# A seven-product FFN: when the operand sums of its second half are split, and how long split weights are held

## The chip, the cores and the metric

The kernel runs on one NeuronCore of a Trainium2 chip. The metric is the device time of one execution in microseconds. One execution was also recorded by the profiler; its "span" is the time from its first to its last instruction on the core.

## The reference

One layer of a hybrid decoder is computed for 2048 prompt tokens and 64 sample tokens, in float32: RMSNorm, a joint input projection, sliding-window attention beside an RWKV-7 recurrence, a gated merge with a residual add, and then the causal ConvFFN with another residual add and a last RMSNorm. The change lies in the FFN alone:

```python
def conv_ffn(h, conv_prev, w_in, cw, cb, w_out):
    T = h.shape[1]
    u = h @ w_in
    gp, vp = u[..., :D_FF], u[..., D_FF:]
    buf = jnp.concatenate([conv_prev.astype(gp.dtype), gp], axis=1)
    c = cb + sum(cw[j] * buf[:, j:j + T] for j in range(CONV_W))
    return (jax.nn.gelu(c, approximate=True) * vp) @ w_out, buf[:, -(CONV_W - 1):]
# x = x + merged @ w_out
# f, conv_new = conv_ffn(rmsnorm(x, norm_ffn), conv_prev, w_ffn_in, ffn_conv_w, ffn_conv_b, w_ffn_out)
# D_MODEL = 1024, D_FF = 2816 (22 tiles of 128), CONV_W = 3
```

## The kernel before, in words

The 2112 tokens are worked in three blocks of 704. Features lie on the 128 partitions and tokens along the free dimension. Each block passes through input projections, attention and recurrence, a merge, and the FFN. Blocks 0 and 2 take the path of `stage_s`, which calls `merge_s` (L1231) and then `ffn_s` (L1307); block 1 takes the plain path `merge` and `ffn`, which the change doesn't touch.

**Precision by splitting.** Every matmul operand is stored as two parts, `hi`, a rounded copy, and `lo`, the value less that copy. `split` (L248) makes them: ScalarE (ACT) casts the value to `hi` (L249), then VectorE (DVE) or GpSimd (POOL) subtracts (L250). `unit` (L234) does the same for a 128 x 1024 weight: a load on SyncE's queue into the pool `wr` (two buffers), the cast by ACT at L241 into the pool `wp` (two buffers), the subtraction by DVE or POOL at L245. `mm3` (L252) multiplies hi by hi, hi by lo and lo by hi: three matmuls for each of the k-tiles, all at L260. A product of four k-tiles is 12 matmuls.

**Background work.** `push` hands a generator to a named stream. `mm3` calls `tick` ahead of the k-tiles whose number is 0, 3 or 6, and a tick advances each stream by one step; a value that the generator yields is a number of ticks to leave out. A product of four k-tiles ticks twice. `drain` runs what is left of a stream.

**Seven products.** In `ffn_s` the normalized input is cut in four: the two halves of its features by the two halves of the tokens (352 each, `FH`). The first token half gives t11 and t12, split into `sa` (a11, a12); the second gives t21 and t22. For each of the 22 feature tiles f, gate and value weights, also cut by halves of the features, are combined so that seven products of four k-tiles do instead of eight: a11 and a12 with the gate weight as it is (`wa`, or in the early loop `unit`), and five others with sums of weights, "quarters" (`quarter`, L1345, tile `wq`, three buffers; the sums, L1327, in tiles `tq` and `rw`), against the operand sums s2, s3, s1, a22 and s4. These five live in the tile `sb`, as parts 0 to 4: t11 (after it has been overwritten), t21, s1, t22 and t12. `p1`, `u2`, `u3` are partial results that DVE adds up out of PSUM.

**Order in a stage.** `merge_s` ends with the out-projection of both token halves, during which `first` makes `sa`. It then pushes `second` (L1281), which takes the norm of the second half and, for each k-tile, forms the operand sums on DVE and POOL, splits part 0, and at last splits parts 1 to 4: 20 splits of 128 x 352 in all, 10 with POOL. `second` is advanced by the ticks of the early loop (L1354): for f = 0 to 5 (`PRE` = 6) the products with a11 and a12, kept in `keep`. `t11` lies in `wq` buffers, `t21` in the tiles `gb` and `cc`, `t22` in `xv`, `s1` in `up` and one of the two buffers of `rw`, `t12` in `early`.

Then the main loop runs over groups of f (`GRP`: one of 2, five of 4). For each f it issues, in this order: for f of 6 and over the a11 product into the bank `bx` (L1382), with a copy `p1` of it by ACT (L1384); the product with s2 (`bw`); if a group has just ended, `behind()` (L1394), which is `ffn_out` (L1204) of that group; the products with s3 (`bz`) and s1 (`by`); for f of 6 and over the a12 product, added into `bx` (L1407); the copy of `c11` to `gb` and the first convolution tap (L1408, L1409); the products with a22 and s4, the convolution (L1194), the gelu (L1425), the product of gate and value (L1430) and the split into `ff`. `ffn_out` of a group of 4 takes four `unit` weights, each for 48 matmuls. `whole` (L1338) makes `wa[f + 1]` near the end of f, in a `wp` buffer.

**What sets the order on the engines.** The program is written with tiles; a planner takes the instructions in the order of the program as their rank, lets one go ahead where by its own estimates of cost the earlier ones aren't ready and a buffer is free, and writes one fixed queue for each engine. On the chip each engine works its queue in order and waits where the data or a buffer isn't there.

Of the kernel before, what the change touches and what calls it, by code (L numbers as in the profile page):

```python
# [26 lines left out]
FH = ((0, 352), (352, 352))  # L27
PRE = 6
# [76 lines left out]
class Kernel:  # L105
# [1125 lines left out]
    def merge_s(self, b, xp, msp, after):  # L1231

        nc = self.nc
        with self.pool("br") as brp:
            x, ms = self.branches(b, xp, brp, msp, brp)
        fp, sap, sbp = after()
# [42 lines left out]
        sb = sbp().tile([P, 5, 4, 2, n], F32R, name="sb")  # L1279

        def second():  # L1281

            part = lambda u, k, t, eng: self.split(sb[:, u, k, 0], sb[:, u, k, 1], t, eng)
            yield from rms(1)
            yield
            for k in range(4):
                normed(t21[k], k, 1)
                normed(t22[k], k + 4, 1)
                nc.vector.tensor_tensor(s1[k], t21[k], t22[k], op=ALU.add)
                nc.gpsimd.tensor_tensor(t21[k], t11[k], t21[k], op=ALU.subtract)  # L1290
                nc.vector.tensor_tensor(t11[k], s1[k], t11[k], op=ALU.subtract)
                part(0, k, t11[k], nc.gpsimd)
                nc.gpsimd.tensor_tensor(t12[k], t12[k], t11[k], op=ALU.subtract)
                yield
            for k in range(4):
                part(1, k, t21[k], nc.vector)
                if k % 2:
                    yield
            for u, t in ((2, s1), (3, t22), (4, t12)):
                for k in range(4):  # L1300
                    part(u, k, t[k], nc.gpsimd if k % 2 else nc.vector)
                yield

        self.push("m", second())
        return x, sa, sb, early

    def ffn_s(self, b, x, sa, sb, early, fp, between, done):  # L1307
        nc = self.nc
# [36 lines left out]
        def quarter(f, u):  # L1345
            if f < FF:
                t = raw[f][u]
                w = q[f, u] = fp.tile([P, 2, 512], F32R, tag="wq", name="wq", bufs=3)
                nc.scalar.copy(w[:, 0], t)  # L1349
                sub(nc.gpsimd, w[:, 1], t, w[:, 0].bitcast(F32))  # L1350
# [3 lines left out]
        for f in range(PRE):  # L1354
# [8 lines left out]
            nc.vector.tensor_tensor(c11, p1, pss[1][:, :n], op=ALU.add)  # L1363
        self.drain("m")
        quarter(0, 1)
        behind = None
        for f0, nf in GRP:
            ff = []
            for u in range(nf):
# [21 lines left out]
                u2 = self.tmp("u2")[:, :n]  # L1391
                nc.vector.tensor_tensor(u2, p1, bw[:, :n], op=ALU.add)
                if behind:
                    behind()  # L1394
                    behind = None
# [9 lines left out]
                nc.vector.tensor_tensor(up[:, n:], u3, by[:, :n], op=ALU.add)  # L1405
                if f >= PRE:
                    self.mm3(bx, wa.pop(f), a12, 0, n, nk=4, wk0=4, start=False)  # L1407
                nc.scalar.copy(gb[:, 2:2 + n], c11)  # L1408
                tap(c[:, :n], c11)  # L1409
                sums(f + 1)  # L1410
# [4 lines left out]
                if last:  # L1415
                    v8 = lambda t: t.rearrange("p (b i) -> p b i", i=8)
                    nc.vector.tensor_tensor(sv[:, :, 2:], v8(u2[:, np_:]), v8(bz[:, np_:n]), op=ALU.add)
                    tap(v8(c[:, npr:]), sv[:, :, 2:])
                whole(f + 1)
                quarter(f + 1, 0)  # L1420
# [173 lines left out]
    def stage_s(self, b, held, ahead=None):  # L1594
# [3 lines left out]
        with ExitStack() as es, ExitStack() as right:  # L1598
# [11 lines left out]

            x, sa, sb, early = self.merge_s(b, xp, msp, after)
            fp = pools[0]
# [29 lines left out]

            self.ffn_s(b, x, sa, sb, early, fp, between, self.final_last(b, x, fp) if last else self.final(b, x, FH))
            if last:
# [111 lines left out]
```

## Time and profile before

| what | value |
|---|---|
| three timed runs | 3622.6, 3636.28, 3649.86 us (median 3636.28) |
| the profiled execution | 3638.56 us |
| its span | 3636.8 us |
| TensorE (PE) matmul, busy | 3285.3 us, 90% of the span, 23544 matmuls |
| weight loads (PEld), busy | 3117.5 us, 86% |
| DVE, ACT, POOL, busy | 2276.3 (63%), 1290.5 (35%), 1398.3 us (38%) |
| mean granted TensorE clock | 0.956 of full |

A row of the timeline gives start in us, length, engine, line, operation, tile written and tiles read, shape and count; in brackets stands the idle time of the engine before it and what ended that. PEld are weight loads, SPq is SyncE's queue, where the loads are issued. In a row of a group of lines the numbers behind the first bar are busy us and mean ns of one, behind the second the idle time before them, by what ended it. A row on a tile gives minimum, median and maximum ns, and first and last start. Matmul records overlap, so their mean length is longer than the step from one to the next. Products into the banks `psd` and `psr` are told apart by what they read: `sa` (a11, a12), `sb` (the five others), `ff` (output products).

### The profile page before, as it was taken

What the parts mean: (1) busy time and instruction counts of PE and PEld (TensorE: products, weight loads), DVE (VectorE), ACT (ScalarE), POOL (GpSimd) and SP (SyncE); (2) the same over time, 40 slices, a digit from 0 to 9 for tenths busy, and PEclk for the clock granted to TensorE, in tenths of its full rate; (3) what the DMA queues carried; (4) which work ended last, traced back from release to release, by engine and by line L of the source; (5) the groups of instructions that cost most, each with busy time, mean ns of one, the idle gap of its engine ahead of it and who ended that gap; (6) DMA issues with size and microseconds to landing.
All of it is one profiled execution on the core that took longest, in us unless ns stands there. A gap on an engine that the chain in (4) does not pass through costs nothing. (4 is left out here: it accounts for less than half of the span.)

```text
span 3636.8 us, 61117 instructions
## 1 busy us (share of the span) xinstructions
PE 3285.3 (90%) x23544; PEld 3117.5 (86%) x23544; DVE 2276.3 (63%) x4739; ACT 1290.5 (35%) x2486; POOL 1398.3 (38%) x1224
## 2 busy tenths in 40 slices
PE   8888899988997899899899899999999997898987
PEld 7887788887896888898888689999999997798887
DVE  6668856579557755555665955564644656855555
ACT  4323533235333433333333432331222323433334
POOL 3443224342256444554344213122212345644445
PEclk9999899999998999999999899999999998999998
DMA  3444465544532312127545434433222463212122
GB/s 129 120 121 132 120 202 151 158 133 118 195 127 87 96 62 67 64 71 224 178 141 164 117 125 166 157 102 103 72 70 70 147 223 105 76 59 69 59 65 80
DMA packets 318708, 429.60 MB, mean 118 GB/s; under 512 B 83664, under 2 KB 242256, under 8 KB 318160
## 3 DMA queue, kind: packets, MB, share of 16 engines
q1 hardware_dynamic: 314256, 419.92, 37.1%
q10 hardware_dynamic: 4160, 5.77, 0.5%
q8 instruction: 186, 3.05, 0.4%
q14 instruction: 106, 0.87, 0.1%
HBM read 328.16 MB, written 98.41 MB: 117 GB/s over the span
## 5 line engine op out<-in xcount | busy, mean ns | idle before, releaser
L260 PE MATMUL psd<-h,wp 128*128 128x384 f32 (+2 forms) x6336 | 1168.8, 338 | 20.1 <-ACT wp L241 7.9
L260 PEld LDWEIGHTS psd<-h,wp 128*128 128x128 f32 x6336 | 1057.0, 196 | 41.3 <-ACT wp L241 8.2
L245 POOL TENSOR_TENSOR wp<-wr,wp 128x1024 fp32r<-128x1024 f32 x182 | 444.3, 2441 | 980.7 <-ACT wp L241 936.4
L260 PE MATMUL psd<-ff,wp 128*128 128x352 f32 (+2 forms) x3168 | 552.5, 331 | 48.9 <-POOL wp L245 23.8
L260 PEld LDWEIGHTS psd<-ff,wp 128*128 128x128 f32 x3168 | 517.3, 192 | 70.0 <-POOL wp L245 29.3
L260 PE MATMUL psd<-o,wp 128*128 128x384 f32 (+1 forms) x3264 | 544.4, 326 | 8.7 <-ACT wp L241 2.5
L260 PEld LDWEIGHTS psd<-o,wp 128*128 128x128 f32 x3264 | 529.6, 190 | 13.2 <-ACT wp L241 2.6
L241 ACT CAST wp<-wr 128x1024 fp32r<-128x1024 f32 x298 | 312.0, 1047 | 553.6 <-PE psd L260 434.0
L1220 DVE TENSOR_TENSOR x<-x,psd 128x352 f32<-128x352 f32 (+2 forms) x288 | 148.4, 518 | 273.5 <-PE psd L260 273.3
L260 PE MATMUL psd<-sb,wq 128*128 128x352 f32 x1584 | 283.5, 328 | 20.4 <-POOL wq L1314 17.5
L260 PEld LDWEIGHTS psd<-sb,wq 128*128 128x128 f32 x1584 | 263.2, 191 | 25.3 <-POOL wq L1314 21.6
L1314 POOL TENSOR_TENSOR wq<-tq,wq 128x512 fp32r<-128x512 f32 x132 | 191.5, 1453 | 205.2 <-ACT wq L1349 205.1
L260 PE MATMUL psr<-sb,wq 128*128 128x352 f32 x1056 | 205.5, 341 | 47.0 <-DVE u L1401 29.9
L260 PEld LDWEIGHTS psr<-sb,wq 128*128 128x128 f32 x1056 | 182.7, 199 | 55.6 <-ACT ff L249 19.1
L1194 DVE SCALAR_TENSOR_TENSOR cc<-gb,pt,cc 128x704 f32<-128x704 f32 (+1 forms) x132 | 182.4, 1382 | 22.0 <-ACT cc L1181 11.7
L245 DVE TENSOR_TENSOR wp<-wr,wp 128x1024 fp32r<-128x1024 f32 x116 | 153.0, 1319 | 52.5 <-ACT wp L241 51.5
L1314 POOL TENSOR_TENSOR wq<-rw,wq 128x512 fp32r<-128x512 f32 x88 | 132.7, 1508 | 67.4 <-ACT wq L1349 67.4
L1314 DVE TENSOR_TENSOR tq<-rw 128x512 f32<-128x512 f32 x88 | 86.8, 990 | 98.9 <-DMA rw<-in_w_fi 85.1
L260 PE MATMUL psr<-sa,wp 128*128 128x352 f32 x768 | 136.1, 324 | 0.7 <-ACT p L1384 0.7
L260 PEld LDWEIGHTS psr<-sa,wp 128*128 128x128 f32 x768 | 125.5, 188 | 1.9 <-ACT p L1384 1.9
L250 DVE TENSOR_TENSOR ff<-cc,ff 128x352 fp32r<-128x352 f32 (+2 forms) x132 | 111.4, 853 | 21.1 <-ACT ff L249 18.9
L844 DVE TENSOR_TENSOR m<-psr,ct 128x512 f32<-128x512 f32 (+2 forms) x88 | 46.0, 542 | 111.4 <-DMA kbd<-kt 55.6
(318 smaller groups left out, 4654.6 us busy)
## 6 DMA issues: line engine op xcount, KB each, us to landing
wr<-in_w_in SPq DMA_DIRECT2D x108, 512.0 KB, 3.8
wr<-in_w_fi SPq DMA_DIRECT2D x100, 512.0 KB, 3.5
wr<-in_w_fo SPq DMA_DIRECT2D x70, 512.0 KB, 3.5
rw<-in_w_fi SPq DMA_DIRECT2D x44, 512.0 KB, 3.5
wr<-in_w_out SPq DMA_DIRECT2D x40, 512.0 KB, 3.5
cm<-md SPq DMA_DIRECT2D x33, 512.0 KB, 4.7
gt<-gd SPq DMA_DIRECT2D x48, 352.0 KB, 4.3
md<-m SPq DMA_DIRECT2D x48, 256.0 KB, 3.2
```

Of the source, the lines that this page charges most:

```text
L241: nc.scalar.copy(w[:, 0], raw)
L245: eng.tensor_tensor(w[:, 1], raw, w[:, 0].bitcast(F32), op=ALU.subtract)
L250: (eng or self.nc.vector).tensor_tensor(lo, src, hi.bitcast(F32), op=ALU.subtract)
L260: nc.tensor.matmul(ps[:, :n], w[:, a, wk * 128:(wk + 1) * 128], x, skip_group_check=not start, start=(start and k == 0 and j == 0), stop=( ...
L844: nc.vector.tensor_tensor(m[:, :kpr], ps[:, :kpr * 128].rearrange("p (c j) -> p c j", j=128), self.cst("maskp").unsqueeze(1).to_broadcast( ...
L1194: nc.vector.scalar_tensor_tensor(c[:, :npr], gb[:, u:u + npr], cw[u], c[:, :npr], op0=ALU.mult, op1=ALU.add)
L1220: nc.vector.tensor_tensor(xv, xv, ps[:, :n], op=ALU.add)
L1314: sub = lambda eng, o, p, q: eng.tensor_tensor(o, p, q, op=ALU.subtract)
```

## The change

Two things change in the two seven-product stages. First, `second` splits only part 0, with DVE instead of POOL, and each k-tile takes two steps with a tick left out after each. The splits of the other four parts become four callables, which `ffn_s` calls around f = 0: part 1 (t21) right behind the early loop, part 2 (s1) behind the s2 product, part 3 (t22) behind the s1 product and part 4 (t12) behind the a22 product; in each, DVE and POOL take turns (t21 was split by DVE alone). Second, where a group has just ended and f is 6 or over, the a12 product, the copy to `gb` and the first tap go ahead of `behind()`, so that `wa[f]` is given up before the group's output products instead of after them.

```diff
@@ merge_s
         sb = sbp().tile([P, 5, 4, 2, n], F32R, name="sb")
+        part = lambda u, k, t, eng: self.split(sb[:, u, k, 0], sb[:, u, k, 1], t, eng)
+
         def second():
-            part = lambda u, k, t, eng: self.split(sb[:, u, k, 0], sb[:, u, k, 1], t, eng)
             yield from rms(1)
             yield
             for k in range(4):
@@
                 nc.gpsimd.tensor_tensor(t21[k], t11[k], t21[k], op=ALU.subtract)
+                yield 1
                 nc.vector.tensor_tensor(t11[k], s1[k], t11[k], op=ALU.subtract)
-                part(0, k, t11[k], nc.gpsimd)
+                part(0, k, t11[k], nc.vector)
                 nc.gpsimd.tensor_tensor(t12[k], t12[k], t11[k], op=ALU.subtract)
-                yield
+                yield 1
+
+        def rest(u, t):
             for k in range(4):
-                part(1, k, t21[k], nc.vector)
-                if k % 2:
-                    yield
-            for u, t in ((2, s1), (3, t22), (4, t12)):
-                for k in range(4):
-                    part(u, k, t[k], nc.gpsimd if k % 2 else nc.vector)
-                yield
+                part(u, k, t[k], nc.gpsimd if k % 2 else nc.vector)
 
         self.push("m", second())
-        return x, sa, sb, early
+        return x, sa, sb, early, [lambda u=u, t=t: rest(u + 1, t) for u, t in enumerate((t21, s1, t22, t12))]
@@ ffn_s
         self.drain("m")
+        parts[0]()
         quarter(0, 1)
@@
                 nc.vector.tensor_tensor(u2, p1, bw[:, :n], op=ALU.add)
+                if f == 0:
+                    parts[1]()
                 if behind:
+                    if f >= PRE:
+                        self.mm3(bx, wa.pop(f), a12, 0, n, nk=4, wk0=4, start=False)
+                        nc.scalar.copy(gb[:, 2:2 + n], c11)
+                        tap(c[:, :n], c11)
                     behind()
                     behind = None
@@
                 nc.vector.tensor_tensor(up[:, n:], u3, by[:, :n], op=ALU.add)
-                if f >= PRE:
+                if f == 0:
+                    parts[2]()
+                if f in wa:
                     self.mm3(bx, wa.pop(f), a12, 0, n, nk=4, wk0=4, start=False)
-                nc.scalar.copy(gb[:, 2:2 + n], c11)
-                tap(c[:, :n], c11)
+                if f < PRE or u:
+                    nc.scalar.copy(gb[:, 2:2 + n], c11)
+                    tap(c[:, :n], c11)
                 sums(f + 1)
@@
+                if f == 0:
+                    parts[3]()
                 whole(f + 1)
```

`stage_s` passes the four callables from `merge_s` on to `ffn_s`.

More of the change, by code (lines that the diff above doesn't have):

```diff
@@ L1290, in second, with ffn_s @@
                 nc.gpsimd.tensor_tensor(t21[k], t11[k], t21[k], op=ALU.subtract)
+                yield 1
                 nc.vector.tensor_tensor(t11[k], s1[k], t11[k], op=ALU.subtract)
-                part(0, k, t11[k], nc.gpsimd)
+                part(0, k, t11[k], nc.vector)
                 nc.gpsimd.tensor_tensor(t12[k], t12[k], t11[k], op=ALU.subtract)
-                yield
+                yield 1
+        def rest(u, t):
             for k in range(4):
-                part(1, k, t21[k], nc.vector)
-                if k % 2:
-                    yield
-            for u, t in ((2, s1), (3, t22), (4, t12)):
-                for k in range(4):
-                    part(u, k, t[k], nc.gpsimd if k % 2 else nc.vector)
-                yield
+                part(u, k, t[k], nc.gpsimd if k % 2 else nc.vector)
         self.push("m", second())
-        return x, sa, sb, early
-    def ffn_s(self, b, x, sa, sb, early, fp, between, done):
+        return x, sa, sb, early, [lambda u=u, t=t: rest(u + 1, t) for u, t in enumerate((t21, s1, t22, t12))]
+    def ffn_s(self, b, x, sa, sb, early, parts, fp, between, done):
         nc = self.nc
@@ L1609, in second @@
                 return right.enter_context(self.pool("sb", side="right"))
-            x, sa, sb, early = self.merge_s(b, xp, msp, after)
+            x, sa, sb, early, ops = self.merge_s(b, xp, msp, after)
             fp = pools[0]
@@ L1641, in between @@
                     self.push("n", parts(self.h))
-            self.ffn_s(b, x, sa, sb, early, fp, between, self.final_last(b, x, fp) if last else self.final(b, x, FH))
+            self.ffn_s(b, x, sa, sb, early, ops, fp, between, self.final_last(b, x, fp) if last else self.final(b, x, FH))
             if last:
```

## The prediction

> **What bounds the kernel now.** I read the granted clock and the busy time by stretch first, then TensorE's timeline in the two stages that the change touches (the seven-product FFN of block 0, from 1087 to about 1577 us, and of block 2, from 3034 us to the end), then what the other engines do at its gaps. The columns of the first fence are: stretch, length, busy time of PE, its weight loads, DVE, ACT and POOL, granted clock, DMA.
>
> ```profile
> core 0: us, PE busy (x) PEld busy (x) DVE busy (x) ACT busy (x) POOL busy (x), PEclk, DMA share, GB/s
> 2682.00:2860.00 178.00, 177.05 (x1104) 176.63 (x1103) 86.84 (x122) 47.17 (x68) 36.27 (x16) 1.00 0.21 69
> 1095.90:1165.00 69.10, 45.08 (x242) 42.16 (x242) 51.74 (x61) 29.95 (x58) 51.81 (x38) 0.85 0.31 99
> 3043.30:3115.00 71.70, 47.65 (x252) 45.98 (x250) 53.42 (x71) 28.79 (x56) 50.02 (x37) 0.79 0.29 96
> 1241.70:1250.30 8.60, 8.60 (x39) 8.60 (x39) 6.19 (x22) 2.72 (x6) 1.68 (x2) 0.67 0.28 83
> 1373.10:1381.60 8.50, 8.42 (x43) 8.42 (x44) 2.25 (x4) 0.00 (x0) 2.36 (x2) 0.80 0.38 125
> 3388.40:3397.70 9.30, 9.24 (x40) 8.97 (x41) 2.96 (x6) 0.97 (x3) 1.53 (x1) 0.68 0.00 0
> 3490.90:3497.80 6.90, 6.74 (x40) 6.50 (x41) 2.87 (x6) 0.94 (x2) 1.54 (x1) 1.00 0.00 0
> ```
>
> The first row is how the kernel runs elsewhere: matmuls back to back, 0.161 us each, full clock. In the next two rows, the start of each seven-product stage, PE works two thirds of the time and at a lowered clock: 242 matmuls x 0.161 = 39 us of work in 69. The last four rows stand behind short waits; three of them ran slow for the whole row.
>
> ```profile
> 1103.06 4.11 PE L260 MATMUL psd<-sa,wp 128*128 128x352 f32 x24 [1.08 <-ACT early L1362]
> 1120.05 1.54 PE L260 MATMUL psd<-sa,wp 128*128 128x352 f32 x4 [12.88 <-ACT wp L241]
> 1123.84 5.32 PE L260 MATMUL psd<-sa,wp 128*128 128x352 f32 x20 [2.25 <-DVE wp L245]
> 1134.81 3.48 PE L260 MATMUL psd<-sa,wp 128*128 128x352 f32 x20 [1.80 <-POOL wp L245]
> 3068.55 1.54 PE L260 MATMUL psd<-sa,wp 128*128 128x352 f32 x4 [14.13 <-ACT wp L241]
> ```
>
> This is the early loop (first-half products of f = 0 to 5). PE has f = 3 behind it at 1107.2 and waits 12.88 us (14.13 in block 2) for the weights of f = 4, then again for their rest and for f = 5. Why:
>
> ```profile
> 1098.22 1.05 ACT L241 CAST wp<-wr 128x1024 fp32r<-128x1024 f32 x1 [0.72 <-PE psd L260]
> 1118.95 1.05 ACT L241 CAST wp<-wr 128x1024 fp32r<-128x1024 f32 x1
> 1122.58 1.21 DVE L245 TENSOR_TENSOR wp<-wr,wp 128x1024 fp32r<-128x1024 f32 x1
> 1123.82 0.33 SPq L240 DMA_DIRECT2D wr<-in_w_fi  x1
> 1129.09 1.04 ACT L241 CAST wp<-wr 128x1024 fp32r<-128x1024 f32 x1
> 1131.94 2.81 POOL L245 TENSOR_TENSOR wp<-wr,wp 128x1024 fp32r<-128x1024 f32 x1
> L245 POOL TENSOR_TENSOR wp<-wr,wp x182: 2330/2398/2987, 14.6 to 3616.3; 128x1024 fp32r<-128x1024 f32 x182
> L250 POOL TENSOR_TENSOR sb<-a,sb x12: 922/1206/1232, 1101.7 to 3066.6; 128x352 fp32r<-128x352 f32 x12
> L250 DVE TENSOR_TENSOR sb<-a,sb x12: 511/1110/1251, 1110.6 to 3069.3; 128x352 fp32r<-128x352 f32 x12
> ```
>
> Between the casts at 1098.22 and 1118.95 ACT, which takes its queue in order, serves nearly all of the 20 splits of `second()`, whose data come from DVE and POOL. (The last three rows give minimum, median and maximum ns.) The next weights pay in turn: f = 5's load goes out when f = 4's raw buffer is read (1122.58 + 1.21 = 1123.8), is cast 5.3 us later, and POOL ends its part at 1134.75.
>
> The second place is the output products of a group, run inside the next group's first f:
>
> ```profile
> L260 PE MATMUL psd<-ff,wp 128*128 128x352 f32 x758 | 136.3, 336 | 16.2 <-POOL wp L245 10.4 <-ACT ff L249 4.8 <-DVE x L1220 0.5
> L260 PE MATMUL psd<-ff,wp 128*128 128x352 f32 x767 | 136.0, 333 | 20.3 <-POOL wp L245 10.7 <-ACT ff L249 8.7 <-DVE ff L250 0.4
> 3296.46 1.45 PE L260 MATMUL psr<-sb,wq 128*128 128x352 f32 x8
> 3300.21 6.99 PE L260 MATMUL psd<-ff,wp 128*128 128x352 f32 x42 [1.21 <-POOL wp L245]
> 3288.08 0.43 PE L260 MATMUL psd<-ff,wp 128*128 128x352 f32 x1 [2.98 <-ACT ff L249]
> 3490.93 6.91 PE L260 MATMUL psd<-ff,wp 128*128 128x352 f32 x39 [2.86 <-ACT ff L249]
> 1240.16 0.63 PE L260 MATMUL psd<-ff,wp 128*128 128x352 f32 x2 [2.72 <-ACT ff L249]
> ```
>
> The first two rows are the groups of lines cut to 1236-1577 us (block 0) and 3188-3528 us (block 2), four such places in each. With one of two `wp` buffers held by `wa[f]`, every new output weight is made only when the last one is used up; PE fills part of that time with products out of order (the 8 at 3296.46) and idles the rest, 10.4 + 10.7 us. The `ff` waits, 4.8 + 8.7 us, are for the activation of the group's last f.
>
> **The change, term by term.**
>
> *Early loop.* `second()` keeps 4 of its 20 splits and takes two ticks for each half step. A product of 12 matmuls takes 2.0 us (42 in 6.99) and ticks twice, so a k now spans 4 us, and 16 splits leave. f = 4's cast then stands behind about four such casts and meets its data: its load is out when POOL has read f = 3's raw buffer (1098.22 + 1.05 + 2.4, about 1102), so its weights are ready near 1110, DVE having four k steps, c11 and this split in its queue. f = 5: load at 1110, cast 5.3 later, 1.0, POOL 2.8: ready near 1119.5 against 1134.75, a gain of 15. If DVE's steps line up one behind another, waiting for POOL and ACT between them, f = 5 is ready only near 1127, a gain of 8.
>
> *f = 0.* The 16 splits come back here, four ahead of each of the last four products. POOL then owes f = 0 its eight splits at 1.2 us, five quarter splits and one operand of `sums(1)`:
>
> ```profile
> L1314 POOL TENSOR_TENSOR wq<-tq,wq 128x512 fp32r<-128x512 f32 x8 | 11.4, 1440 | 5.1 <-ACT wq L1349 5.1
> L1314 POOL TENSOR_TENSOR tq<-wr,tq 128x512 f32<-128x512 f32 x3 | 4.4, 1462 | 7.6 <-DVE tq L1314 5.4 <-issue 1.5 <-POOL wp L245 0.7
> ```
>
> 8 x 1.2 + 5 x 1.44 + 1.46 = 18.3 us against five products, 10 us, of PE; only the 3.5 us of f = 5 run ahead. Behind these splits stand POOL's quarters and, on SP, the load of f = 1's `rw`: s1 sits in one of that tag's two buffers until `parts[1]` has read it. But f = 0 waits on POOL already, and f = 1 on the activation chain (1.95 us, next row), so not all is new: I charge 4 us a block (0 to 9).
>
> ```profile
> 1157.30 3.01 PE L260 MATMUL psr<-sb,wq 128*128 128x352 f32 x11 [1.95 <-ACT ff L249]
> ```
>
> Both together: 15 - 4 = 11 us in block 0, 13 in block 2 (its first wait is 1.2 longer), 24 in all. Cross-check: moving part 0 to DVE and sharing t21 gives POOL two splits fewer, 51.8 - 2.4 = 49.4 us of POOL in a stretch of 69 - 11 = 58, 85% full against 75% now. A full POOL allows 20 and 24; the worst is 8 - 9, a loss of 1 each.
>
> *Output weights.* The a12 product goes ahead of `behind()`, so both buffers serve the four output weights. One weight feeds 8 us of matmuls (48) and takes 1.05 + 2.4 to make, so the 21.1 us go but for about one: 20. The products that filled these places run afterwards and lose nothing.
>
> *Activation wait.* The a12 product (2.0 us) now stands before the output products. It needs `wa`, there already, and p1 copied off the same bank:
>
> ```profile
> 3283.11 0.44 ACT L1384 COPY p<-psr 128x352 f32<-128x352 f32 x1
> 3286.16 0.79 ACT L1425 ACTIVATE cc<-cc 128x704 f32<-128x704 f32 x1 [2.61 <-DVE cvs L1200]
> ```
>
> The copy ends at 3283.55, where a12 would begin (the output products began at 3283.50), and 3 us ahead of the gelu that PE really waits for. So a12 covers 2.0 of 2.98, 2.87 and 2.86: 6.0 of 8.7 in block 2, and 4.8 - 0.7 = 4.1 in block 0. Together 10. Against it: the copy to gb and the first tap (0.44 + 0.65 us of ACT) move ahead and can delay that gelu; half of it at 8 places, 4.
>
> *Clock.* Behind waits of 2.4 to 2.9 us the rows lose (1 - clock) x length: 2.8, 1.7 and 3.0 us. Behind 1.2 us 42 matmuls took 6.99, full speed. The waits left are below that, so these 7.5 go. [...] Here the clock was 0.68 behind 2.87 us, and 1.00 behind 2.86, so the measurement decides and the price is chance: between 0 and 10.
>
> Sum: 24 + 20 + 10 - 4 + 7.5 = 57.5 us. The profiled execution took 3638.56 (span 3636.8 and 1.8 around it): 3581. The median of the runs, 3636.28, lies 2.3 below it, so I say 3579. The bounds added up: at least 6 (early -2; 12 of the weight waits, if the products that filled them meet a wait of 1.2 at each of eight places; 4 of the `ff` waits, if p1 comes 0.8 late; the gelu a full 1.0 late at each, -8; clock 0), at most 87 (44, 21, 12 if the early tap costs nothing, 10).
>
> **The rivals.**
> 1. *POOL and DVE are in effect one engine, so the early splits only move* (chance 0.20). For: a split takes DVE 0.51 us at best and 1.11 in the median, POOL 0.92 and 1.21. The two together were busy 103.5 us in the 69.1; squeezed, both lengthen. Then the early term is nothing and the boundaries give 33.5: 3603. Against: POOL stood idle 17 of those 69 us. [...]
> 2. *The boundaries give half*, since what filled them must run later behind POOL (0.08): 24 + 17 = 41 us less 8 of new waits, 3603.
> 3. *The planner already does it*: it fixes each queue's order from its own estimates, may issue a12 or the splits where they stood before, and nothing moves (0.04): 3636.
> 4. *Slower: u3 behind the activation in every f* (0.07). In the later f of a group a22 waits for the DVE addition u3, queued behind the split of the last activation:
>
> ```profile
> 3259.71 2.17 PE L260 MATMUL psr<-sb,wq 128*128 128x352 f32 x12 [1.85 <-DVE u L1401]
> 3560.52 2.93 PE L260 MATMUL psr<-sb,wq 128*128 128x352 f32 x12 [1.85 <-DVE u L1401]
> L260 PE MATMUL psr<-sb,wq 128*128 128x352 f32 x301 | 56.5, 331 | 8.5 <-DVE u L1401 7.1 <-ACT wq L1349 1.2
> L260 PE MATMUL psr<-sb,wq 128*128 128x352 f32 x301 | 56.5, 333 | 10.8 <-DVE u L1401 10.8
> ```
>
> It costs 1.85 us, and 0.8 more where the clock falls (2.93 for 2.17). The two group rows, cut as above, hold 17.9 us of it, some ten waits; f = 2 to 21 of two blocks are 40 f. The edit reorders taps, splits and copies around it; if the planner then puts u3 there in the other 30, that is 30 x 2.65 = 80 us, less 57.5: 3659. It outweighs the gain from 22 f on. Against: groups repeat each other closely now, and u = 1 to 3 keep their text.
>
> **How the numbers follow.** Forecast 0.61, centre 3579, own range 3560 to 3600. With rivals 1 and 2 at 3603 and the bounds of the early term, 3550 to 3615 leaves out 3 and 4 and the tails. Three runs of before spread by 0.4% either way, so 1% (36 us, 3600) is about what can be told. Faster by over 1%: nearly all of the forecast and a third of 1 and 2, 0.69. Within 1%: the rest of these and rival 3, 0.24. Slower: rival 4, 0.07.
>
> **What would show it.** Right: no PE wait over 5 us for `wp` between f = 3 and f = 4; f = 5 starting about 25 us after the second rms instead of 39; the `psd<-ff` rows' wait for POOL `wp` near 1 and for `ff` near 3 us a block. Wrong: new waits for `sb` or `wq` in f = 0 of over 9 us; a12 waiting for p1; more u3 waits than ten; or an early loop as long as before with DVE and POOL both full.

## The result, and the profile after

The changed kernel took 3584.28 us in the median of four runs (3580.55 to 3588.09), the kernel before 3634.24 beside it: a ratio of 0.986, 95% interval 0.9821 to 0.9899. It is 50 us faster. Its profiled execution took 3588.09 us (span 3586.3, against 3636.8). One recorded execution below, the first of the kernel with the splits alone, took 6136.44 us where its nine others took 3610 to 3622, and no reading rests on it.

First the busy time by stretch, before and then after. The first two rows of each fence are the groups of block 0 and block 2, from the first output product of f0 = 2 to the first one of the last group, f0 = 18; the last two rows are the early stretches, from the first matmul on `sa` to the first output product of group 0. Columns as in the prediction.

```profile
core 0: us, PE busy (x) PEld busy (x) DVE busy (x) ACT busy (x) POOL busy (x), PEclk, DMA share, GB/s
1235.70:1627.90 392.20, 356.82 (x2104) 343.70 (x2104) 218.70 (x333) 140.27 (x262) 187.73 (x114) 0.98 0.20 66
3188.30:3579.50 391.20, 353.54 (x2089) 343.35 (x2088) 221.09 (x388) 138.62 (x253) 176.41 (x111) 0.97 0.19 61
1086.70:1165.10 78.40, 52.21 (x287) 48.77 (x287) 58.13 (x76) 33.00 (x62) 54.27 (x39) 0.87 0.31 101
3033.90:3114.70 80.80, 54.75 (x287) 52.79 (x286) 58.51 (x86) 31.74 (x60) 52.08 (x38) 0.79 0.29 98
```

```profile
1236.20:1608.60 372.40, 345.39 (x2093) 339.01 (x2091) 216.18 (x330) 140.15 (x260) 180.78 (x113) 0.99 0.22 70
3159.00:3530.70 371.70, 345.75 (x2077) 340.38 (x2076) 225.40 (x381) 137.39 (x247) 178.47 (x111) 0.98 0.20 64
1092.60:1161.60 69.00, 51.73 (x286) 48.41 (x286) 57.35 (x74) 31.77 (x60) 51.44 (x35) 0.93 0.30 98
3008.10:3082.80 74.70, 57.96 (x286) 55.06 (x286) 63.88 (x89) 31.60 (x60) 52.43 (x36) 0.82 0.30 98
```

The early stretches are 9.4 and 6.0 us shorter (by the instructions at their ends), 15.4 together. The groups are 19.8 and 19.5 us shorter, but one a12 product (1.93 us) has left each of these stretches for the time just ahead of it, so 35.4 us are gained. From the first output product of group 0 to that of f0 = 2, that product taken off, 2.7 us are lost (70.6 to 72.6 us in block 0, 73.5 to 74.2 in block 2); all the rest of the kernel gains 2.2 (5.9 lost ahead of the first stage and 6.6 gained between the two, where no kernel differs, and 1.6 gained behind the groups of block 2). Together 50.3 us; the spans differ by 50.5.

What TensorE waits for in the groups, after (groups of lines, cut to 1236-1608.5 and to 3158.9-3530.7 us):

```profile
L260 PE MATMUL psd<-ff,wp 128*128 128x352 f32 x768 | 123.9, 322 | 0.0
L260 PE MATMUL psd<-sb,wq 128*128 128x352 f32 x564 | 102.4, 329 | 10.3 <-POOL wq L1312 10.3
L260 PE MATMUL psr<-sa,wp 128*128 128x352 f32 x363 | 64.8, 328 | 2.2 <-ACT p L1383 2.2
L260 PE MATMUL psr<-sb,wq 128*128 128x352 f32 x384 | 70.2, 332 | 9.8 <-DVE u L1407 8.9 <-ACT wq L1347 0.8
L323 PE MATMUL psc<-ct,acc 128*128 128x1 f32 x12 | 1.7, 254 | 4.7 <-DVE acc L302 4.7
L260 PE MATMUL psd<-ff,wp 128*128 128x352 f32 x768 | 125.0, 324 | 1.2 <-ACT ff L249 0.8 <-DVE ff L250 0.4
L260 PE MATMUL psr<-sa,wp 128*128 128x352 f32 x362 | 66.9, 335 | 7.8 <-ACT p L1383 7.8
L260 PE MATMUL psr<-sb,wq 128*128 128x352 f32 x384 | 70.2, 333 | 17.0 <-DVE u L1407 17.0
```

The waits of the output products, 16.2 and 20.3 us, are down to 0.0 and 1.2. Three other waits are larger: a12 for `p1` (2.2 and 7.8 us), a22 for `u3` (8.9 and 17.0), and in block 0 the next block's normalization, whose matmuls (L323) stand among the output products and wait 4.7 us for DVE's sum of squares; before, they waited for nothing. The timeline after shows the first of these, at the place where a group's output products begin:

```profile
3344.75 0.79 ACT L1436 ACTIVATE cc<-cc 128x704 f32<-128x704 f32 x1 [2.51 <-DVE cc L1197]
3345.53 0.44 ACT L1383 COPY p<-psr 128x352 f32<-128x352 f32 x1
3346.02 3.89 PE L260 MATMUL psr<-sa,wp 128*128 128x352 f32 x12 [3.63 <-ACT p L1383]
3349.95 0.45 ACT L1398 COPY gb<-psr 128x352 f32<-128x352 f32 x1 [2.38 <-PE psr L260]
```

ACT runs the gelu of the group's last f first and the copy of `p1` behind it. The a12 product adds into the bank that this copy reads, so PE waits 3.63 us for the copy, and its 12 matmuls then take 3.89 us instead of about 2.1. The copy to `gb` comes only after the product, 4.4 us behind the gelu's end.

The early loop after (timeline; POOL, ACT, DVE, SP's queue and PE for the weights of f = 4 and f = 5):

```profile
1105.24 2.59 POOL L245 TENSOR_TENSOR wp<-wr,wp 128x1024 fp32r<-128x1024 f32 x1 [0.42 <-ACT wp L241]
1107.86 11.08 SPq L240 DMA_DIRECT2D wr<-in_w_fi  x2
1113.62 1.04 ACT L241 CAST wp<-wr 128x1024 fp32r<-128x1024 f32 x1
1114.71 0.95 PE L260 MATMUL psd<-sa,wp 128*128 128x352 f32 x4 [3.00 <-ACT wp L241]
1117.37 1.22 DVE L245 TENSOR_TENSOR wp<-wr,wp 128x1024 fp32r<-128x1024 f32 x1
1118.64 5.55 PE L260 MATMUL psd<-sa,wp 128*128 128x352 f32 x20 [2.99 <-DVE wp L245]
1124.49 1.04 ACT L241 CAST wp<-wr 128x1024 fp32r<-128x1024 f32 x1
1129.12 2.63 POOL L245 TENSOR_TENSOR wp<-wr,wp 128x1024 fp32r<-128x1024 f32 x1
1131.81 3.48 PE L260 MATMUL psd<-sa,wp 128*128 128x352 f32 x20 [1.48 <-POOL wp L245]
```

The 12.88 us wait ahead of f = 4 is down to 3.00. f = 5 starts 39.2 us after the stage's first matmul (1092.58), against 48.1 before. But there is slack left in the chain: DVE takes up f = 4's part 2.7 us after the cast has ended, POOL f = 5's part 3.6 us after its cast.

### The profile page after: what moved, and what is told of

It is laid out like the page before. It is cut to its first block, busy times and chain, and to the rows that moved or that the text cites. A ratio compares the mean times of both kernels' runs of the same rounds, so it can differ in the third digit from the quotient of the medians.

```text
span 3586.3 us, 61118 instructions
## 1 busy us (share of the span) xinstructions
PE 3271.3 (91%) x23544; PEld 3112.6 (87%) x23544; DVE 2291.2 (64%) x4743; ACT 1293.0 (36%) x2486; POOL 1396.3 (39%) x1220
## 5 line engine op out<-in xcount | busy, mean ns | idle before, releaser
L260 PE MATMUL psd<-ff,wp 128*128 128x352 f32 (+2 forms) x3168 | 527.4, 325 | 15.6 <-ACT ff L249 4.4
L260 PEld LDWEIGHTS psd<-ff,wp 128*128 128x128 f32 x3168 | 508.8, 189 | 24.1 <-ACT ff L249 5.8
L260 PE MATMUL psd<-sb,wq 128*128 128x352 f32 x1584 | 287.0, 331 | 15.4 <-POOL wq L1312 12.0
L260 PEld LDWEIGHTS psd<-sb,wq 128*128 128x128 f32 x1584 | 266.6, 194 | 20.7 <-POOL wq L1312 16.1
L260 PE MATMUL psr<-sb,wq 128*128 128x352 f32 x1056 | 201.4, 339 | 53.8 <-DVE u L1407 34.2
L260 PE MATMUL psr<-sa,wp 128*128 128x352 f32 x768 | 139.1, 331 | 10.6 <-ACT p L1383 10.6
L250 DVE TENSOR_TENSOR ff<-cc,ff 128x352 fp32r<-128x352 f32 (+2 forms) x132 | 118.9, 915 | 20.1 <-ACT ff L249 18.9
L1312 POOL TENSOR_TENSOR tq<-wr,tq 128x512 f32<-128x512 f32 x44 | 66.3, 1507 | 137.3 <-DVE tq L1312 87.6
```

The costliest lines, as they stand in the source:

```text
L250: (eng or self.nc.vector).tensor_tensor(lo, src, hi.bitcast(F32), op=ALU.subtract)
L260: nc.tensor.matmul(ps[:, :n], w[:, a, wk * 128:(wk + 1) * 128], x, skip_group_check=not start, start=(start and k == 0 and j == 0), stop=( ...
L1312: sub = lambda eng, o, p, q: eng.tensor_tensor(o, p, q, op=ALU.subtract)
```

## The experiments

The table gives the median of each kernel and what its trace says of the two stages, block 0 / block 2: the early loop (first matmul on `sa` to the end of f = 5's products), the early stretch (to the first output product of group 0), and the rest (from there to the end of the stage's last output product). All are read off TensorE's timelines. Each ratio is to the kernel before, run beside that kernel.

| kernel | us | ratio, 95% | early loop | early stretch | rest |
|---|---|---|---|---|---|
| before | 3634.24 | | 51.6 / 54.4 | 78.4 / 80.8 | 498.1 / 507.8 |
| changed | 3584.28 | 0.9821-0.9899 | 42.7 / 45.3 | 69.0 / 74.8 | 482.2 / 489.3 |
| changed, again | 3581.9 | 0.9842-0.9872 | 46.6 / 45.1 | 71.2 / 73.3 | 482.4 / 488.8 |
| splits alone | 3616.34 | 0.9922-0.9953 | 42.7 / 43.9 | 69.1 / 74.3 | 494.5 / 504.5 |
| a12 alone | 3596.59 | 0.9863-0.9926 | 54.4 / 55.7 | 81.0 / 82.5 | 480.4 / 485.6 |
| a12's last k-tile behind | 3594.59 | 0.9863-0.9912 | 45.3 / 45.1 | 71.3 / 73.3 | 485.9 / 489.2 |
| a12 in its own bank | 3574.48 | 0.9787-0.9854 | 42.7 / 46.4 | 69.1 / 73.6 | 477.3 / 479.2 |
| a22 as well | 3572.07 | 0.9807-0.9848 | 46.6 / 45.1 | 72.4 / 74.9 | 473.3 / 475.0 |
| operands not split | 3570.54 | 0.98-0.9843 | 39.2 / 39.1 | 67.5 / 64.6 | 478.6 / 486.3 |
| no pacing | 3595.77 | 0.9855-0.9918 | 47.7 / 47.7 | 74.1 / 74.7 | 483.3 / 486.7 |
| no pacing, again | 3585.37 | 0.9857-0.9894 | 46.1 / 47.6 | 72.3 / 75.6 | 483.7 / 486.0 |
| raw loads of f = 0 later | 3585.86 | 0.9862-0.989 | 35.1 / 35.2 | 73.4 / 69.8 | 485.2 / 485.4 |

**The two parts one at a time.** My theory was that the parts act in different places, the splits in the early stretch and a12 in the groups, and add up. Rivals 1 and 2 of the prediction each have one of them give nothing or half. One kernel has only the first part, all the hunks on the operand splits, and leaves a12 where it was before:

```diff
                 yield 1
-                part(0, k, t11[k], nc.gpsimd)
+                part(0, k, t11[k], nc.vector)
...
+        def rest(u, t):
...
+        parts[0]()
```

> Only the first part: the splits of parts 1 to 4 called around f = 0, part 0 on DVE, two ticks for a half step; the a12 product where it was. Theory 'two separate gains': 13 us less than before (8 to 18), the early stretches 69 and 75 us as in the changed kernel, the waits for POOL wp in the groups back at 21 us. Rival 'POOL and DVE are one engine and the splits only move': within 4 us of before, which the changed trace already speaks against for the early stretch (9 and 6 us less) but not for the f behind it (2.7 us more).

The other is the kernel before with a12, its copy and its tap moved:

```diff
                 if behind:
+                    if f >= PRE:
+                        self.mm3(bx, wa.pop(f), a12, 0, n, nk=4, wk0=4, start=False)
+                        nc.scalar.copy(gb[:, 2:2 + n], c11)
+                        tap(c[:, :n], c11)
                     behind()
```

> Only the second part of the change: the a12 product, the gb copy and the tap ahead of the group's output products; the operand splits as in the kernel before. The changed kernel's trace gives the group stretches of the two blocks 35.5 us less. Theory 'two separate gains': this kernel keeps all of that, 36 us less than before (32 to 40), with the waits of the output products for POOL wp gone and the early stretch as long as before (78 and 81 us). Rival 'the gains depend on each other' (the planner's order of the groups changed because the early stretch did): less than 25 us.

The splits alone gave 20 us (3616.34 against 3636.77 beside it), a12 alone 40 (3596.59), both a little more than expected. For its trace, the first kernel was recorded once more:

> The kernel with the first part of the change alone, the moved and paced splits, once more, for its trace. If the two parts of the change don't meet in the early loop, the stretch up to f=5's weights is 39 to 40 us in both blocks, as in the whole change, and the waits for output weights between f=3 and f=4 are still there, 7 us and more a place. If the part alone leaves the early loop at 48 us, its 20 us come from elsewhere, from f=0 or the groups.

It took 3615.78 us. Its early stretches, 69.1 and 74.3 us, are those of the whole change. Its rest is close to before (3.6 and 3.3 us shorter), and its groups of lines, cut to 1224-1617 and 3167-3560 us, still have the waits for the output weights (10.0 and 10.8 us over four places, as before; the 7 us a place in the expectation was my slip):

```profile
L260 PE MATMUL psd<-ff,wp 128*128 128x352 f32 x781 | 136.1, 329 | 13.2 <-POOL wp L245 10.0 <-ACT ff L249 2.2 <-DVE ff L250 0.7
L260 PE MATMUL psd<-ff,wp 128*128 128x352 f32 x774 | 140.0, 338 | 20.4 <-POOL wp L245 10.8 <-ACT ff L249 9.1 <-DVE ff L250 0.4
```

In the trace of a12 alone it is the other way round: early stretches of 81.0 and 82.5 us, the rest shorter by 17.7 and 22.2, where rival 2 had 17 for both. Its output products (groups of lines, cut to 1251.2-1619 and 3181.6-3550.6 us) wait for no weight:

```profile
L260 PE MATMUL psd<-ff,wp 128*128 128x352 f32 x768 | 125.3, 325 | 0.0
L260 PE MATMUL psd<-ff,wp 128*128 128x352 f32 x768 | 124.0, 322 | 1.2 <-ACT ff L249 0.8 <-DVE ff L250 0.4
```

So the parts act where the theory put them. The sum of the two, 60 us, is 10 more than the whole change gave; with intervals of 6 us either side on the one and 11 on the other, that can't be told from none. (In the traces the two stages are 22.7 and 35.6 us shorter, the whole change 49.8.)

**Buffer or cover?** a12 ahead of the output products does two things: it gives up a weight buffer, and it gives PE 2 us of work while the activation ends. This kernel was meant to hold the buffer and keep most of the cover.

```diff
-                        self.mm3(bx, wa.pop(f), a12, 0, n, nk=4, wk0=4, start=False)
-                        nc.scalar.copy(gb[:, 2:2 + n], c11)
-                        tap(c[:, :n], c11)
+                        self.mm3(bx, wa[f], a12, 0, n, nk=3, wk0=4, start=False)
                     behind()
+                    if f >= PRE:
+                        self.mm3(bx, wa.pop(f), a12, 0, n, k0=3, nk=1, wk0=7, start=False)
...
```

> The changed kernel, but the last of the four k-tiles of each early a12 product (3 of 12 matmuls) stands behind the group's output products, so that the weight buffer is held as before while three quarters of the product still cover the activation wait. Theory 'it is the buffer': the waits for POOL wp come back, about 21 us more than the changed kernel and up to 5 more of lowered clock, so 3605 to 3610. Rival 'it is the cover, 2 us of work put ahead of the wait': within 6 us of the changed kernel, 3584 to 3590.

It came out at 3594.59, between the two, and settles little: the planner issued the three matmuls right behind the first output weight (at 1251.73, 3173.70 and 3269.18 us, for example), so the buffer was held for one weight only, and the waits for POOL's `wp` came to 3.2 and 2.5 us a block, not 10. Its two stages together are only 4.4 us longer than the changed kernel's. How the gain divides between buffer and cover was not shown by a run.

**The wait for p1.** In the changed kernel a12 waits for ACT's copy because both use one bank. Here a12 gets a bank of its own, and DVE adds it to `p1`:

```diff
-                        self.mm3(bx, wa.pop(f), a12, 0, n, nk=4, wk0=4, start=False)
-                        nc.scalar.copy(gb[:, 2:2 + n], c11)
-                        tap(c[:, :n], c11)
+                        bx2 = self.bank()
+                        self.mm3(bx2, wa.pop(f), a12, 0, n, nk=4, wk0=4)
+                        nc.vector.tensor_tensor(gb[:, 2:2 + n], p1, bx2[:, :n], op=ALU.add)
+                        tap(c[:, :n], gb[:, 2:2 + n])
```

> The changed kernel with the early a12 product in a PSUM bank of its own, added to p1 by DVE straight into gb, so that it needn't wait until ACT has copied p1 off the shared bank. In the changed trace a12 waits 2.2 us (block 0) and 7.8 us (block 2) for that copy, which ACT makes behind the gelu of the group's last f at two places. Theory 'the rest of the activation wait turned into a wait for p1': these 10 us go at most down to the wait for ff that then shows, which a12 covers by 2 us; 5 to 10 us less than the changed kernel, 3574 to 3579. Rival 'PE waits for the same activation chain either way': the wait for ff grows by what the wait for p1 shrinks, within 3 us of the changed kernel.

3574.48 us, 10 below the changed kernel, as expected; the rest of the stages is 4.9 and 10.1 us shorter. The intervals of the two ratios overlap, so the times alone don't prove the 10 us; the two stages together are 16 us shorter in the trace (1099 against 1115 us in the first trace of the changed kernel and 1116 in the second). The groups of lines, cut to 1166.8-1640 and to 3083-3563 us:

```profile
L260 PE MATMUL psr<-sa,wp 128*128 128x352 f32 x384 | 67.2, 324 | 0.6 <-ACT p L1383 0.6
L260 PE MATMUL psr<-sb,wq 128*128 128x352 f32 x480 | 86.3, 327 | 14.7 <-DVE u L1408 10.6 <-ACT ff L249 2.7 <-ACT wq L1347 1.2
L260 PE MATMUL psr<-sa,wp 128*128 128x352 f32 x384 | 67.3, 323 | 0.0
L260 PE MATMUL psr<-sb,wq 128*128 128x352 f32 x480 | 90.9, 339 | 26.3 <-DVE u L1408 17.8 <-ACT ff L249 8.5
```

The p1 waits of 10 us are down to 0.6. The largest wait left is the last row's, a22 for `u3`. The same remedy was tried on it:

```diff
-                self.mm3(bz, q[f, 3], a22, 0, n, nk=4, wk0=0, start=False)
+                bv = self.bank("r")
+                self.mm3(bv, q[f, 3], a22, 0, n, nk=4, wk0=0)
-                nc.vector.tensor_tensor(gb[:, 2 + n:2 + npr], u2[:, :np_], bz[:, :np_], op=ALU.add)
+                nc.vector.tensor_tensor(gb[:, 2 + n:2 + npr], u3[:, :np_], bv[:, :np_], op=ALU.add)
```

> The kernel with a12's product in a PSUM bank of its own (3574), and now the a22 product too: it starts a bank of its own instead of adding to the one that DVE reads for u3, and DVE adds it to u3. In the trace of the former kernel TensorE idles 12.7 us ahead of the a22 products between 1000 and 1700 us for DVE's u3. If that wait is the bank alone, it goes in both blocks, some 25 to 34 us with the block at 3000 us, and the time is 3540 to 3555. If the wait only moves, because the a22 weights (POOL's splits) or the next bank come no earlier, the rows for POOL's wq grow by about what the u3 rows lose and the time is within 8 us of 3574.

3572.07 us, 2.4 less and not distinguishable: the rival held. The groups of lines (1166.8-1640, then 3083-3563 us):

```profile
L260 PE MATMUL psr<-sb,wq 128*128 128x352 f32 x480 | 85.5, 324 | 3.6 <-POOL wq L1312 3.6
L260 PE MATMUL psd<-sb,wq 128*128 128x352 f32 x709 | 129.0, 331 | 20.6 <-DVE up L1412 10.8 <-POOL wq L1312 9.8
L260 PE MATMUL psr<-sb,wq 128*128 128x352 f32 x476 | 86.9, 327 | 9.3 <-POOL wq L1312 7.9 <-ACT wq L1347 1.4
L260 PE MATMUL psd<-sb,wq 128*128 128x352 f32 x708 | 129.1, 332 | 13.4 <-POOL wq L1312 7.7 <-DVE up L1412 5.6
```

The 28.4 us of `u` waits (10.6 and 17.8) are gone, and the 11.2 us of `ff` in the same rows. But POOL's `wq` now has 29.0 us in these rows, against 10.6 in the kernel with a12 alone in a bank, and DVE's `up` 16.4 against 3.1. All idle time ahead of the `sb` products went from 54.7 to 46.9 us: 7.8 of the 39.6 were gained, and the rest of the stages is 4.0 and 4.2 us shorter. The early stretches of this execution were longer by 4.6, so the time shows even less. So `u3` was only the last of several things that end at nearly the same time. With 3572 and 3574 us, against 3582 and 3584 of the changed kernel, these two versions with banks of their own are the fastest here that compute the whole reference.

**Why the early loop gained 9 us a block and not 15.** Two theories: DVE and POOL are still too busy with the operand splits; or the raw loads, one after another through two buffers, set when f = 5's weights come. The first kernel rounds the five operands once; it leaves out their low parts and doesn't compute the reference, and stands here for its times alone:

```diff
-        part = lambda u, k, t, eng: self.split(sb[:, u, k, 0], sb[:, u, k, 1], t, eng)
+        part = lambda u, k, t, eng: nc.scalar.copy(sb[:, u, k, 0], t)
```

> The changed kernel with the five operand sums of the second half (the sb operands) rounded once instead of split in two: the copies to the high part are made by ScalarE, and the low parts and their subtractions by DVE and POOL, 20 of each kind a block, are left out; the three matmuls of a weight tile use the high part twice, so TensorE has as many matmuls as before. This leaves out the low part of those operands. If the load of DVE and POOL still bounds the early stretch and the first f (my reading of why the first part of the change gave 9 us up to f=5's weights and not 15), the stretch from the first matmul on sa to the first output product of group 0 falls from 69.0 and 74.8 us to 60 to 65 us in each block, and the time is 14 to 25 us below the changed kernel: about 3560 to 3570. If the chain of f=5's weights (raw loads, sums, casts, one after the other) bounds it whatever else DVE and POOL do, the stretches keep to within 3 us and the time is within 6 us of the changed kernel: 3578 to 3590.

3570.54 us, 14 below the changed kernel. Its timeline for f = 5's weights:

```profile
1114.82 1.04 ACT L241 CAST wp<-wr 128x1024 fp32r<-128x1024 f32 x1
1116.37 2.36 POOL L245 TENSOR_TENSOR wp<-wr,wp 128x1024 fp32r<-128x1024 f32 x1
```

POOL starts 0.5 us after the cast and ends at 1118.73, 32.0 us after the first matmul at 1086.75: 16 us earlier in the stage than before. So load is one cause. The early stretch fell as expected only in block 2 (64.6); in block 0 f = 0 then ran into later waits (2.98 us for `u3`, 1.83 for `wq`) and the stretch stayed at 67.5. The other kernel changes the order of the raw loads alone, the last two lines standing behind the loop:

```diff
-            if f > 2:
-                (lambda: load(0), lambda: sums(0), lambda: quarter(0, 0))[f - 3]()
+            if f == 5:
+                load(0)
...
+        sums(0)
+        quarter(0, 0)
```

> The changed kernel with the raw loads of f=0's quarter weights, their sums and their first cast moved from between f=3, f=4 and f=5 of the early loop to f=5 and behind the loop. If the order of the raw loads is the other half of why f=5's weights came only 9 us earlier (f=5's raw load waits for a buffer behind the loads of f=0), the stretch up to f=5's last matmul falls from 42.7 and 45.3 us to 34 to 38 us, and f=0's work behind it grows by as much or more, 26 to 29 us becoming 33 to 42: the time is 0 to 15 us above the changed kernel. If that order costs nothing, the stretch up to f=5 keeps to within 2 us and only f=0 grows.

```profile
1119.11 3.79 PE L260 MATMUL psd<-sa,wp 128*128 128x352 f32 x22 [0.29 <-POOL wp L245]
1127.63 0.81 PE L260 MATMUL psd<-sb,wq 128*128 128x352 f32 x2 [4.73 <-ACT wq L1347]
```

f = 5 now starts 31.4 us after the first matmul (1087.75) and the early loop ends at about 35.2 us in both blocks, but f = 0 pays it back (38.3 and 34.6 us): the two early stretches add up to 143.2 us, against 143.8 in the changed kernel, and 3585.86 us is 4 above the changed kernel beside it. So either cause alone can delay f = 5, and freeing f = 5 alone is worth nothing: up to the first output product the weights of f = 4, 5 and 0 all have to pass DVE and POOL, and of the kernels here only the one that takes work off these two shortened the sum (132.1 us).

**Pacing or moving?** The first part moves splits and also spreads the normalization's steps over more ticks. This kernel takes the spreading back:

```diff
                 nc.gpsimd.tensor_tensor(t21[k], t11[k], t21[k], op=ALU.subtract)
-                yield 1
...
-                yield 1
+                yield
```

> The changed kernel with the two paced stops in the loop over the four tiles of the second normalization taken back to the one plain stop of the kernel before; the splits stay where the change puts them, after the early loop and in f=0. If the gain of the early stretch comes from moving the splits, the time is that of the changed kernel within 4 us (3580 to 3588). If it comes from the pacing, which spreads the normalization's work over the early loop's weight groups, the time up to f=5's weights goes from 39 to 40 us back towards 48 to 49 us in each block, and the whole is 10 to 18 us above the changed kernel (3594 to 3602).

Its 3595.77 us read as 11 us for the pacing, but the early stretches were only 5.0 us longer, 74.1 and 74.7. The rest of the difference lay between the two stages (1371.6 us from block 0's last output product to block 2's first matmul on `sa`, against 1364.2), where no kernel differs. So both were run once more, side by side:

> The changed kernel itself once more, beside the next two on one chip. Its stages without the change (the stretch between the two FFN blocks of the trace, 1364.2 us from the end of block 0's products to the first matmul on sa of block 2, and 1364 to 1372 us in the other kernels' traces) tell how far the time of one execution wanders for no cause in the change. If that wandering is a few us an execution, the median is 3580 to 3588 again.

> The kernel without the paced stops once more. In its first trace the early stretches were 74.1 and 74.7 us, against 69.0 and 74.8 of the changed kernel: 5 us, all in block 0, while its time was 11 us above. If the pacing is worth what the trace shows, the median is 4 to 6 us above the changed kernel's in this comparison; if it is worth what the times show, 10 us and more.

Now 3581.9 and 3585.37: 3.5 us apart, with early stretches of 144.5 and 147.9 us together. The trace was the better measure of the two: pacing is worth 3 to 5 us of the 15 (the two traces of the changed kernel differ by 0.7 in this sum), and what is left falls to the other hunks on the splits, which no run takes apart.

## Why the prediction was right, and where its steps were not

The time, 3584.28 against 3579, and the sign came out as forecast. By the prediction's terms, for the profiled execution:

| term | forecast | measured |
|---|---|---|
| early loop and f = 0 | 11 + 13 = 24 | 9.4 + 6.0 = 15.4 |
| output weights | 20 | 21.1 |
| activation wait less the early tap | 10 - 4 = 6 | 3.4 |
| clock in the groups | 7.5 | 5.1 |
| other waits in the groups | | -4.4 |
| matmul time in the groups beyond the clock | | 10.2 |
| f = 2 to 5, all the rest | | -2.7, +2.2 |
| sum | 57.5 | 50.3 |

The sum is close in part by luck: 10.2 us came from matmul time that no term held, and they made up for most of what the early loop and the activation wait fell short. The forecast sum also has a slip: block 2's wait is 1.2 us longer than block 0's, which makes its early term 12.2 and not 13.

*Early loop.* The mechanism was right; the step that failed is "f = 5: load at 1110, cast 5.3 later, 1.0, POOL 2.8: ready near 1119.5". Counted from the stage's first matmul, that is 32.8 us for f = 5's weights; it was 39.2 (40.2 in block 2), a gain of 8.9 and 9.2. From the second rms to f = 5 it was 30.0 us (1101.8 to 1131.8), not the 25 that I gave as a sign. The load of f = 4 went out when forecast (15.3 us). Then DVE took up f = 4's part 2.7 us late, the next load and cast took 5.9 us instead of 5.3, and POOL began 3.6 us behind the cast. PE's waits for f = 4 are 3.00 and 2.99 us in the rows above, of 12.88 and 2.25 before. This is the bound that I had named, DVE's steps in line behind one another, and it should have been the value. Behind it stands a premise that was wrong: "16 splits leave". The planner took most of them back into the early loop. Of 20 operand casts, 11 stood ahead of f = 4's weight cast, not four, and 19 ended before f = 5's weights (the answer on the tile `sb` for ACT, 1092.6 to 1131.8 us):

```profile
L249 ACT CAST sb<-a x12: 480/484/487, 1102.9 to 1128.0; 128x352 fp32r<-128x352 f32 x12
L249 ACT CAST sb<-s x4: 480/486/488, 1105.4 to 1124.1; 128x352 fp32r<-128x352 f32 x4
L249 ACT CAST sb<-early x3: 482/485/485, 1111.9 to 1119.4; 128x352 fp32r<-128x352 f32 x3
```

So, as I read the trace, the gain is that the weights' casts came between the splits, more than that the splits went elsewhere; no run separates the two. That is a piece of rival 3, which I had priced at no gain at all. It fits f = 0 too, charged 4 us a block, which gained 0.5 in block 0 and lost 3.1 in block 2: few splits were left to pay there.

*Rival 1*, POOL and DVE as one engine, was half right. The kernel with the operands not split had f = 5's weights at 32.0 us in block 0, as forecast for the change, so without the splits' load on the two engines the other 7 us come too (an earlier raw load also brought them, and lost them again in f = 0). In the early loop after, DVE's nine subtractions for `sb` up to 1131.8 us mean 1.23 us (9.0 and 2.1 us by their source), where the ten before had a mean of 0.93 and 0.51 at best. In these rows the length goes with POOL's work: before, five of them from 1112.63 to 1119.72 us, beside a busy POOL, took 1.24 or 1.25 us each, and three from 1120.84 to 1122.22 us, with POOL idle, 0.51; the longest after, 2.67 us from 1129.46, ran beside POOL's weight part of 2.63 us from 1129.12. What lies behind that no run shows, and the gain of 9 us doesn't tell either, since it can come from the order of the work alone.

*Output weights.* Forecast 20, and both POOL `wp` waits, 10.4 and 10.7 us, are off the rows. What had filled these places ran later at little cost: the `u` and `wq` waits of the `sb` products in the groups went from 35.5 us (9.4 + 7.1 + 1.6 + 4.7 + 12.7) to 37.0 (10.3 + 8.9 + 0.8 + 17.0). The rows before, cut to 1235.7-1627.9 and 3188.3-3579.5 us, and last the normalization's, from the first cut:

```profile
L260 PE MATMUL psd<-sb,wq 128*128 128x352 f32 x565 | 101.1, 325 | 9.4 <-POOL wq L1314 9.4
L260 PE MATMUL psr<-sb,wq 128*128 128x352 f32 x384 | 71.4, 330 | 9.0 <-DVE u L1401 7.1 <-ACT wq L1349 1.6
L260 PE MATMUL psd<-sb,wq 128*128 128x352 f32 x565 | 102.0, 329 | 4.7 <-POOL wq L1314 4.7
L260 PE MATMUL psr<-sb,wq 128*128 128x352 f32 x384 | 71.8, 333 | 12.7 <-DVE u L1401 12.7
L323 PE MATMUL psc<-ct,acc 128*128 128x1 f32 x12 | 2.0, 286 | 0.0
```

*Activation.* The step that failed: the p1 copy "ends at 3283.55, where a12 would begin ... and 3 us ahead of the gelu that PE really waits for". At five of the eight places the planner put the copy behind the gelu. So the `ff` wait went (12.7 of 13.5 us), and a12 then waited itself, 10.0 us against 0.7 (7.3 of them at the last two places of block 2): 3.4 are left. At block 0's first place the `ff` wait of 2.72 us only changed its name: PE now waits 2.76 us there for the next block's normalization, part of the 4.7 us of the L323 row, which every kernel here with the early a12 shows (2.7 to 4.7 us). In return the 4 us for an early tap were not paid, since the copy to `gb` too came after the gelu. The kernel with a bank of its own confirms the cause: the wait for p1 went, and the median fell by 10 us. The prediction had named a12 waiting for `p1` as a sign of error.

*Clock.* The clocks of the rows are rounded to 0.01, too coarse for this. From the trace's own records, (1 - clock) x length over the group stretches is 18.8 us before (8.5 + 10.2) and 13.7 after (5.1 + 8.5): 5.1 less, of the 7.5 forecast. PE's idle time there (length less busy) went from 73.0 to 53.0 us, 20.1 less and not the 24.5 of the two terms above: other waits, L323's above all, took 4.4 back. The other 15.4 of the 35.4 us are time in which PE was busy, three times what the clock explains. What the sum lacked: a wait cost more here than its idle time. By the starts of the matmuls, the first two steps behind a wait of PE, beyond that idle time and 0.161 us a step, take some 0.25 us together: 16.1 us at 62 waits before, 9.6 at 38 after, 6.5 less. (The profile models the ends of matmuls, so part of this may be how it counts idle time.) The remaining 4 us I can't assign. Nor are the waits left all shorter than 1.2 us, as the term had it: the row of 3.89 us behind the p1 wait of 3.63 had a granted clock of 0.50, so a12's new wait cost clock too.

*Rival 4*, u3 behind the activation in every f, came only in small: the `u` waits of the whole page went from 29.9 to 34.2 us. Its sign, "more u3 waits than ten", did appear: in the group stretches there are 15 of them after and 10 before, four of the new ones of 1.1 us in block 2, one in each group. They cost 6 us in all (19.8 to 25.9) and not 80.

## What to carry to other kernels

Moving an operation in the program's text moves it on the chip only as far as the planner's rank and estimates let it: count in the trace where it went before you credit the move. A product that is moved ahead to cover a wait must itself be free of that wait; here it shared a PSUM bank with a copy that queued behind the very activation it should have covered, and a bank of its own was worth another 10 us in the median. When the last of several nearly equal waits is removed, price the next one: 40 us of waits for `u3` and the activation went, and 8 of them were gained. And count the waits as well as their length: fewer waits, 38 for 62 in the groups here, also shortened the matmul time between them, by some 0.25 us a wait.

## What the runs showed of the hardware that I had not expected

The clock behind nearly equal short waits differed between two executions of the changed kernel. The same 20 matmuls of f = 5 in block 0, first in the changed kernel's second trace, then in its first one shown above (1131.81, 3.48 us):

```profile
1132.35 6.16 PE L260 MATMUL psd<-sa,wp 128*128 128x352 f32 x20 [1.89 <-POOL wp L245]
```

At 0.161 us a step 20 matmuls are 3.2 us, at twice that 6.4. They took 6.16 us behind a wait of 1.89, and 3.48 behind 1.48; in the kernel before, 3.48 behind 1.80; the granted clock was 0.52 over the first of these rows and 1.00 over the other two. Behind 2.86 us in the kernel before it was 1.00 too, so the length of the last wait alone didn't set it; what did, no run here shows. The stages that no kernel changed also wander: from block 0's last output product to block 2's first matmul on `sa` it was 1364.2 to 1371.6 us over the traces, and the changed kernel itself stood at both ends (1364.2 and 1371.1). PE was idle for as long in both (68.1 and 67.1 us), but the same 10250 matmuls kept it busy for 1296.2 us in the one and 1304.0 in the other, at a mean granted clock of 0.98 and 0.97. With differences of 5 to 10 us, the stretch in the trace told more than a median of four runs.
